# Opening of a two-block network on one core: modulation of four feature tiles and the sum of squares moved to TensorE

## The chip, the cores and the metric

The kernel runs on one core of one Trainium2 chip. The metric is the device time of one execution in microseconds. A core has TensorE (matrix products, with a separate stream of weight loads), VectorE, ScalarE, GpSimd, SyncE (SP, which here only issues loads) and 16 DMA engines that fill the on-chip memory. Products land in PSUM, eight banks of 512 fp32 columns.

## The reference, cut to what matters

Two transformer-like blocks in sequence on 256 tokens of 1024 features, fp32. Only the start of the first block is touched by the change:

```python
cond = silu(c)                                     # c: (1, 1024)
mod = (cond @ w_ada + b_ada).reshape(b, 6, d)      # w_ada: (1024, 6144)
shift1, scale1, gate1, shift2, scale2, gate2 = [mod[:, i] for i in range(6)]
hn = rmsnorm(x, norm1_g) * (1 + scale1) + shift1   # x: (1, 256, 1024)
proj = hn @ w_in                                   # split into q, k, v, index q, k, weights, gates
```

Everything behind it (index scores and top-k attention, stick-breaking attention, an expert layer that picks among 16384 rows, and the whole second block) is the same before and after.

## The kernel before, in words

Activations are held feature-major: eight tiles of 128 features by 256 tokens. Weights come in chunks of 128x1024 fp32 (512 KB) through four buffers `wraw`. Each chunk is split by `weights` (L92) into a high part, a ScalarE copy (L98), and a low part, a subtract on VectorE or GpSimd (L100); activations are split likewise. A product is then made of three: high x high, high x low, low x high. A scheduler orders each engine's instructions when the program is built, from the dependences, the order of the code and its own estimate of times; `issue_after` adds an order between two instructions of one engine. On the chip each engine follows its list.

The opening is in `first_mixer` (L284). The row c is loaded and spread over 128 partitions by two products with a column of ones (L251); after a Silu it is `cond`, 128x1024. x comes in four loads (L301), ScalarE squares it (L303), VectorE adds the squares up (L305 to L307), and one fp32 product with a matrix of ones sums over the partitions (L314). From it come `ms` and `rstd` (L326, and L169 to L174), and `xr` = x times `rstd` (L336): the first pair of tiles on VectorE, three pairs on GpSimd.

The modulation rows are made one tile of 128 output features at a time: `ada_one` (L260) loads a 128x1024 block of the transposed `w_ada` and VectorE multiplies it with `cond` and sums along the row (L266). Tile k needs two of them, row 8+k for the scale and row k for the shift. They use four buffers, two for even and two for odd tiles; those of the odd tiles share their memory (`bias1`) with the squares. VectorE then adds `b_ada` (L270) and makes the scale `gs` (L389), ScalarE makes `hn` and `y` (L393), and VectorE the low part of `hn` (L395).

The products against `w_in` are in pieces (L361, L363), so that they can start with the first tile. The string `ORDER` lists the steps: "a" makes the next tile of `hn` and multiplies it with all chunks that are there, "w" brings one of nine chunks for index q, k and their weights, and multiplies it with all tiles that are there, "v" brings one of four chunks of the value weights, each covering two tiles. `LOWS` says which of the 13 chunks have their low part made on VectorE (v) or GpSimd (g). SP issues the loads in the order of the steps and waits whenever a buffer isn't free. When all eight tiles are done, ScalarE copies the sums out (L425 to L432), and the index scores begin (L609).

Of the kernel before, what the change touches and what calls it, by code (L numbers as in the profile page):

```python
# [9 lines left out]
FT = mybir.dt.float32  # L10
# [3 lines left out]
AF = mybir.ActivationFunctionType  # L14
OP = mybir.AluOpType
# [4 lines left out]
T = 256  # L20
D = 1024
KT = 8
EPS = 1e-6
NEG = -3.0e38
TAKEN = -3.4e38
ORDER = "wwawaavavwwawavwwaawv"
LOWS = "vgvgvgvvvvvgv"
EXP_LN = 6
# [42 lines left out]
class Net:  # L71
# [15 lines left out]
    def load(self, dst, src):  # L87

        with self.tc.issue_after(self.last_load.ins) if self.in_turn else ExitStack():
            self.last_load = self.nc.sync.dma_start(dst, src)  # L90
# [152 lines left out]
    def load_cond(self, pool):  # L243

        nc = self.nc
        row = pool.tile([1, D], FT, name="crow")
        nc.sync.dma_start(row, self.ap["c"])
        self.cond = pool.tile([128, D], FT, name="cond")
        pss = [self.ps([128, 512], "mm") for _ in range(2)]
        for z, ps in enumerate(pss):  # L250
            nc.tensor.matmul(ps, self.ones[0:1, :], row[:, 512 * z:512 * z + 512], start=True, stop=True)  # L251

        def finish():
            for z, ps in enumerate(pss):
                self.last_act = nc.scalar.activation(self.cond[:, 512 * z:512 * z + 512], ps, AF.Silu)
            self.condd = self.dram.tile([1, D], FT, name="condd")
            nc.scalar.dma_start(self.condd, self.cond[0:1, :])
        return finish

# [24 lines left out]
    def first_mixer(self):  # L284
        nc, tc, ap = self.nc, self.tc, self.ap
        with ExitStack() as es:
# [10 lines left out]
            self.table = self.act_table(SILU)  # L297
            cond = self.load_cond(A)
            sq = P.tile([128, KT, T], FT, name="sqs", tag="bias1")
            for k in range(0, KT, 2):  # L300
                nc.sync.dma_start(x[:, k:k + 2], ap["x"][:, k:k + 2])  # L301
                with tc.issue_after(self.table):
                    high = nc.scalar.activation(sq[:, k:k + 2], x[:, k:k + 2], AF.Square)  # L303
                if k % 4:
                    nc.vector.tensor_add(sq[:, k - 2:k], sq[:, k - 2:k], sq[:, k:k + 2])  # L305
            nc.vector.tensor_add(sq[:, :2], sq[:, :2], sq[:, 4:6])
            pair = nc.vector.tensor_add(sq[:, 0], sq[:, 0], sq[:, 1])  # L307
            with tc.issue_after(high.ins):
# [3 lines left out]
            nc.scalar.dma_start(self.b_ada, self.ap["b_ada"])  # L312
            ps = self.ps([128, T], "sm")
            nc.tensor.matmul(ps, self.ones, sq[:, 0], start=True, stop=True)  # L314
            r = P.tile([128, T], FT, name="rstd")
            n1 = Scratch(P.tile([128, 3 * T], FT, name="norm1", tag="kx"))
            ms = n1.tile([128, T], FT, name="ms")
            rows = [Scratch(P.tile([128, 2 * D], FT, name=f"ada{i}", tag=t)) for i, t in enumerate(("sgb", "bias1"))]

            def ada_row(k, j):  # L320
                self.ada_one(A, j, rows[k % 2].tile([128, D], FT, name="ada", bufs=2))

            with tc.issue_after(pair.ins):
                ada_row(0, 8)
            with tc.issue_after(self.last_ada.ins):
                mean = nc.vector.tensor_scalar(ms, ps, 1.0 / D, EPS, op0=OP.mult, op1=OP.add)  # L326
            with tc.issue_after(mean.ins):
                ada_row(0, 0)
            with tc.issue_after(self.last_ada.ins):
                self.rsqrt(n1, r, ms, [128, T])  # L330
# [3 lines left out]
            xr = P.tile([128, KT, T], FT, name="xr", tag="sga")  # L334
            for k in range(0, KT, 2):
                (nc.gpsimd if k else nc.vector).tensor_tensor(  # L336
                    xr[:, k:k + 2], x[:, k:k + 2], r[:, None, :].to_broadcast([128, 2, T]), op=OP.mult)

# [8 lines left out]
            f = F.__enter__()  # L347
# [6 lines left out]
            vacc = [self.ps([128, 512], "acc") for _ in range(2)]  # L354
            nlow = iter(LOWS)

# [25 lines left out]
            for e in ORDER:  # L382
                if e == "a":
                    k = known
                    if k:
                        ada_row(k, 8 + k)
                        ada_row(k, k)
                    self.ada_end(k, k + 1)
                    nc.vector.scalar_tensor_tensor(self.gs[:, 0, k:k + 1], self.mod[:, 8 + k:9 + k],  # L389
                                                   self.vecs[:, 0, k:k + 1], bg[:, k:k + 1], op0=OP.mult, op1=OP.add)  # L390
# [14 lines left out]
                with tc.issue_after(norm_exp.ins), tc.issue_after(self.last_rsqrt.ins):  # L405
                    w = self.weights(ap["w_in"][len(first) if e == "w" else 9 + c], next(nlow),
                                     spare.pop() if e == "w" else None)
# [1031 lines left out]
def _col(v):  # L1439
    return v.reshape(-1, 128).T  # L1440
# [10 lines left out]
def prepare(inputs):  # L1451
    i = {k: np.asarray(v) for k, v in inputs.items()}
    ar = np.arange
    o = {}
    o["x"] = i["x"][0].T.reshape(8, 128, 256).transpose(1, 0, 2)
    o["mem"] = i["mem_2"][0].T.reshape(8, 128, 256).transpose(1, 0, 2)
    o["c"] = i["c"]
    o["w_ada"] = i["w_ada"][0].T.reshape(48, 128, 1024)
    o["b_ada"] = _col(i["b_ada"][0])
    o["vecs"] = np.stack([_col(v) for v in (  # L1460
# [57 lines left out]
```

## Time and profile before

| what | value |
|---|---|
| median of 3 runs | 1452.14 us (1450.41 to 1454.54) |
| the profiled execution | 1451.56 us, span 1449.8 us |
| TensorE busy | 1382.8 us (95%) |
| VectorE busy | 1102.9 us (76%) |
| ScalarE busy | 756.3 us (52%) |
| GpSimd busy | 151.3 us (10%) |

All times of the rows are counted from the start of the span. "Busy" is the share of time in which an engine has an instruction at work; a product and the weight load of the next one overlap. In a row of the timeline the first number is the start, the second the time from the start of the first to the end of the last instruction merged into it, then engine, line, operation, output<-inputs, shape and count. In a row of the table of stretches stand its bounds and length, the busy time (and count of instructions) of TensorE's products, its weight loads, VectorE, ScalarE and GpSimd, the granted clock of TensorE, the share of the DMA engines and what they moved in GB/s. In the timeline, what stands in square brackets is how long the engine had been idle, and what ended that.

### The profile page before, as it was taken

What the parts mean: (1) busy time and instruction counts of PE and PEld (TensorE: products, weight loads), DVE (VectorE), ACT (ScalarE), POOL (GpSimd) and SP (SyncE); (2) the same over time, 40 slices, a digit from 0 to 9 for tenths busy, and PEclk for the clock granted to TensorE, in tenths of its full rate; (3) what the DMA queues carried; (4) which work ended last, traced back from release to release, by engine and by line L of the source; (5) the groups of instructions that cost most, each with busy time, mean ns of one, the idle gap of its engine ahead of it and who ended that gap; (6) DMA issues with size and microseconds to landing.
All of it is one profiled execution on the core that took longest, in us unless ns stands there. A gap on an engine that the chain in (4) does not pass through costs nothing. (4 is left out here: it accounts for less than half of the span.)

```text
span 1449.8 us, 28871 instructions
## 1 busy us (share of the span) xinstructions
PE 1382.8 (95%) x11584; PEld 1326.8 (92%) x11584; DVE 1102.9 (76%) x2082; ACT 756.3 (52%) x1358; POOL 151.3 (10%) x64
## 2 busy tenths in 40 slices
PE   4989899999898999999999999999999999899997
PEld 2879799899898999999999999999999879799996
DVE  7797988549999888999856556665557796777776
ACT  4546664455445555555554444444445465655555
POOL 3100000018995000000000000000000000000001
PEclk9999999999999999999999999999999999999998
DMA  7766776655555545545566666776664444266662
GB/s 278 268 202 230 267 243 200 207 186 156 169 186 161 168 153 166 166 151 171 152 207 221 198 189 192 240 233 201 186 188 141 148 123 157 74 189 191 192 193 94
DMA packets 76234, 269.51 MB, mean 186 GB/s; under 512 B 8970, under 2 KB 11202, under 8 KB 75460
## 3 DMA queue, kind: packets, MB, share of 16 engines
q1 hardware_dynamic: 71426, 257.99, 55.6%
q10 hardware_dynamic: 4674, 9.69, 2.0%
q8 instruction: 90, 1.47, 0.4%
q14 instruction: 44, 0.36, 0.1%
HBM read 265.01 MB, written 4.21 MB: 186 GB/s over the span
## 5 line engine op out<-in xcount | busy, mean ns | idle before, releaser
L98 ACT ACTIVATE wh<-wraw 128x1024 fp32r<-128x1024 f32 x431 | 456.3, 1061 | 522.8 <-PE ps_acc L130 244.1
L100 DVE TENSOR_TENSOR wl<-wraw,wh 128x1024 fp32r<-128x1024 f32 x384 | 470.3, 1227 | 253.9 <-ACT wh L98 251.1
L129 PE MATMUL ps_acc<-c,wh 128*128 128x256 f32 x1024 | 286.6, 280 | 0.0
L130 PE MATMUL ps_acc<-c,wh 128*128 128x256 f32 x1024 | 286.5, 280 | 0.0
L131 PE MATMUL ps_acc<-c,wl 128*128 128x256 f32 x1024 | 286.5, 280 | 0.0
L131 PE MATMUL ps_mm<-hn,wl 128*128 128x256 f32 x680 | 190.1, 280 | 9.8 <-DVE wl L100 7.1
L131 PE MATMUL ps_acc<-hn,wl 128*128 128x256 f32 x696 | 192.5, 277 | 4.7 <-POOL wl L100 4.7
L129 PE MATMUL ps_mm<-hn,wh 128*128 128x256 f32 x680 | 192.6, 283 | 2.7 <-ACT wh L98 2.6
L129 PE MATMUL ps_acc<-hn,wh 128*128 128x256 f32 x696 | 193.9, 280 | 0.0
L129 PEld LDWEIGHTS ps_acc<-c,wh 128*128 128x128 f32 x1024 | 192.5, 188 | 0.1
L131 PEld LDWEIGHTS ps_acc<-c,wl 128*128 128x128 f32 x1024 | 192.5, 188 | 0.0
L130 PEld LDWEIGHTS ps_acc<-c,wh 128*128 128x128 f32 x1024 | 192.5, 188 | 0.0
L130 PE MATMUL ps_acc<-hn,wh 128*128 128x256 f32 x696 | 192.4, 277 | 0.0
L130 PE MATMUL ps_mm<-hn,wh 128*128 128x256 f32 x680 | 189.5, 279 | 0.0
L131 PEld LDWEIGHTS ps_mm<-hn,wl 128*128 128x128 f32 x680 | 128.2, 189 | 11.6 <-DVE wl L100 8.6
L100 POOL TENSOR_TENSOR wl<-wraw,wh 128x1024 fp32r<-128x1024 f32 x47 | 131.8, 2826 | 56.4 <-ACT wh L98 56.2
L131 PEld LDWEIGHTS ps_acc<-hn,wl 128*128 128x128 f32 x696 | 130.8, 188 | 5.4 <-POOL wl L100 5.4
L129 PEld LDWEIGHTS ps_mm<-hn,wh 128*128 128x128 f32 x680 | 128.9, 190 | 5.2 <-ACT wh L98 3.3
L130 PEld LDWEIGHTS ps_acc<-hn,wh 128*128 128x128 f32 x696 | 130.7, 188 | 0.2 <-DVE hn L281 0.2
L129 PEld LDWEIGHTS ps_acc<-hn,wh 128*128 128x128 f32 x696 | 130.4, 188 | 0.4 <-ACT hn L280 0.2
L130 PEld LDWEIGHTS ps_mm<-hn,wh 128*128 128x128 f32 x680 | 128.5, 189 | 0.2
L1404 POOL TENSOR_TENSOR big<-big 128x512 f32<-128x512 f32 x4 | 5.0, 1265 | 981.8 <-DVE big L1401 981.8
(484 smaller groups left out, 2770.9 us busy)
## 6 DMA issues: line engine op xcount, KB each, us to landing
wraw<-in_peer_u_dram SPq DMA_DIRECT2D x128, 512.0 KB, 4.0
wraw<-in_peer_v_dram SPq DMA_DIRECT2D x128, 512.0 KB, 4.4
wraw<-in_w_in_dram SPq DMA_DIRECT2D x70, 512.0 KB, 4.8
wraw<-in_ffn_up_dram SPq DMA_DIRECT2D x44, 512.0 KB, 3.6
wraw<-in_ffn_down_dram SPq DMA_DIRECT2D x22, 512.0 KB, 3.6
ada<-in_w_ada_dram SPq DMA_DIRECT2D x16, 512.0 KB, 6.0
wraw<-in_w_out_dram SPq DMA_DIRECT2D x16, 512.0 KB, 4.6
wraw<-in_peer_wq_dram SPq DMA_DIRECT2D x16, 512.0 KB, 3.6
```

The source lines that it names most:

```text
L98: nc.scalar.activation(h, raw, AF.Copy)
L100: (nc.vector if eng == "v" else nc.gpsimd).tensor_tensor(l, raw, h.bitcast(FT), op=OP.subtract)
L129: mm(out, a[0], b[0], start=first, stop=False, **kw)
L130: mm(out, a[0], b[1], start=False, stop=False, **kw)
L131: self.last_mm = mm(out, a[1], b[0], start=False, stop=last, **kw)
L1404: nc.gpsimd.tensor_tensor(xf[:, tb, cs], xt[:, tb, cs], fg[:, cs], op=OP.mult)
```

## The change

- The eight modulation rows of tiles 0 to 3 (the constant `ADA_PE`) are made on TensorE: their blocks of `w_ada` are stored in the other orientation, and each row is eight accumulating fp32 products, with the block as weights and one column of `cond_col`, repeated 64 times, as the moving operand. The results stand in one PSUM bank, 64 columns each; VectorE reads the first column. Tiles 4 to 7 stay on VectorE.
- The squares are summed by eight fp32 products with the matrix of ones that accumulate in the same bank (its first 256 columns, which tiles 2 and 3 use afterwards), in place of VectorE's adds and one product. The squares use another buffer (`hm1`).
- The conditioning row comes twice: as columns (128x8) on ScalarE's queue, and as a load that repeats it over 128 partitions, behind x on SP's queue, in place of two products.
- GpSimd's share goes to VectorE: the low parts of four chunks, and three pairs of `xr`, which are now made one pair at a time in the even "a" steps.
- `ORDER` is another one.

```diff
--- before.py
+++ after.py
@@ -23,8 +23,8 @@
 EPS = 1e-6
 NEG = -3.0e38
 TAKEN = -3.4e38
-ORDER = "wwawaavavwwawavwwaawv"
-LOWS = "vgvgvgvvvvvgv"
+ORDER = "awwawawawwvvaawwvwaav"
+ADA_PE = 4
 EXP_LN = 6
 SILU = 18
 PLAN = "ijjaavaasvqvqvksskkssksqssrgrqsssrgss0gr1rggr0rrrgrg1rg20g31rg2rrg3rrgg23rg"
@@ -243,19 +243,22 @@
     def load_cond(self, pool):
 
         nc = self.nc
-        row = pool.tile([1, D], FT, name="crow")
-        nc.sync.dma_start(row, self.ap["c"])
+        col = pool.tile([128, KT], FT, name="ccol")
+        nc.scalar.dma_start(col, self.ap["c_col"])
+        self.cond_col = pool.tile([128, KT], FT, name="cond_col")
+        with self.tc.issue_after(self.table):
+            nc.scalar.activation(self.cond_col, col, AF.Silu)
         self.cond = pool.tile([128, D], FT, name="cond")
-        pss = [self.ps([128, 512], "mm") for _ in range(2)]
-        for z, ps in enumerate(pss):
-            nc.tensor.matmul(ps, self.ones[0:1, :], row[:, 512 * z:512 * z + 512], start=True, stop=True)
+        c = self.ap["c"]
+
+        def load():
+            nc.sync.dma_start(self.cond, bass.AP(tensor=c.tensor, offset=c.offset, ap=[[0, 128], [1, D]]))
 
         def finish():
-            for z, ps in enumerate(pss):
-                self.last_act = nc.scalar.activation(self.cond[:, 512 * z:512 * z + 512], ps, AF.Silu)
+            self.last_act = nc.scalar.activation(self.cond, self.cond, AF.Silu)
             self.condd = self.dram.tile([1, D], FT, name="condd")
             nc.scalar.dma_start(self.condd, self.cond[0:1, :])
-        return finish
+        return load, finish
 
     def ada_one(self, pool, j, w=None):
         nc = self.nc
@@ -295,46 +298,58 @@
             self.upper = P.tile([128, 128], FT, name="upper")
             nc.vector.tensor_scalar(self.upper, self.relx[:, 128:], 0.0, None, op0=OP.is_gt)
             self.table = self.act_table(SILU)
-            cond = self.load_cond(A)
-            sq = P.tile([128, KT, T], FT, name="sqs", tag="bias1")
+            load_cond, cond = self.load_cond(A)
+            rows = [Scratch(P.tile([128, 2 * D], FT, name=f"ada{i}", tag=t)) for i, t in enumerate(("sgb", "bias1"))]
+            ps = self.ps([128, 2 * T], "sm")
+            mods = ps.rearrange("p (a b) -> p a b", b=64)
+
+            def mod_at(k, j):
+
+                return (k + 2) % 4 * 2 + j // 8
+
+            def ada_row(k, j):
+                w = rows[k % 2].tile([128, D], FT, name="ada", bufs=2)
+                if k >= ADA_PE:
+                    return self.ada_one(A, j, w)
+                self.load(w, self.ap["w_ada"][j])
+                for i in range(KT):
+                    with tc.issue_after(bank.ins):
+                        nc.tensor.matmul(mods[:, mod_at(k, j)], w[:, i * 128:i * 128 + 128],
+                                         self.cond_col[:, i:i + 1].to_broadcast([128, 64]),
+                                         start=k == 2 and j == 10 and i == 0, stop=i == KT - 1, skip_group_check=True)
+
+            sq = P.tile([128, KT, T], FT, name="sqs", tag="hm1")
             for k in range(0, KT, 2):
                 nc.sync.dma_start(x[:, k:k + 2], ap["x"][:, k:k + 2])
                 with tc.issue_after(self.table):
                     high = nc.scalar.activation(sq[:, k:k + 2], x[:, k:k + 2], AF.Square)
-                if k % 4:
-                    nc.vector.tensor_add(sq[:, k - 2:k], sq[:, k - 2:k], sq[:, k:k + 2])
-            nc.vector.tensor_add(sq[:, :2], sq[:, :2], sq[:, 4:6])
-            pair = nc.vector.tensor_add(sq[:, 0], sq[:, 0], sq[:, 1])
+                for i in (k, k + 1):
+                    with tc.issue_after(bank.ins) if i else ExitStack():
+                        m = nc.tensor.matmul(ps[:, :T], self.ones, sq[:, i], start=i == 0, stop=i == KT - 1,
+                                             skip_group_check=True)
+                    bank = bank if i else m
+            load_cond()
             with tc.issue_after(high.ins):
                 cond()
             self.table = self.act_table(EXP_LN, self.last_act)
             nc.scalar.dma_start(self.vecs, self.ap["vecs"])
             nc.scalar.dma_start(self.b_ada, self.ap["b_ada"])
-            ps = self.ps([128, T], "sm")
-            nc.tensor.matmul(ps, self.ones, sq[:, 0], start=True, stop=True)
             r = P.tile([128, T], FT, name="rstd")
             n1 = Scratch(P.tile([128, 3 * T], FT, name="norm1", tag="kx"))
             ms = n1.tile([128, T], FT, name="ms")
-            rows = [Scratch(P.tile([128, 2 * D], FT, name=f"ada{i}", tag=t)) for i, t in enumerate(("sgb", "bias1"))]
-
-            def ada_row(k, j):
-                self.ada_one(A, j, rows[k % 2].tile([128, D], FT, name="ada", bufs=2))
-
-            with tc.issue_after(pair.ins):
-                ada_row(0, 8)
-            with tc.issue_after(self.last_ada.ins):
-                mean = nc.vector.tensor_scalar(ms, ps, 1.0 / D, EPS, op0=OP.mult, op1=OP.add)
+            mean = nc.vector.tensor_scalar(ms, ps[:, :T], 1.0 / D, EPS, op0=OP.mult, op1=OP.add)
+            ada_row(0, 8)
+            ada_row(0, 0)
             with tc.issue_after(mean.ins):
-                ada_row(0, 0)
-            with tc.issue_after(self.last_ada.ins):
                 self.rsqrt(n1, r, ms, [128, T])
             norm_exp = self.last_exp
             bg = P.tile([128, KT], FT, name="bg")
             nc.vector.scalar_tensor_tensor(bg, self.b_ada[:, 8:16], 1.0, self.vecs[:, 0], op0=OP.add, op1=OP.mult)
             xr = P.tile([128, KT, T], FT, name="xr", tag="sga")
-            for k in range(0, KT, 2):
-                (nc.gpsimd if k else nc.vector).tensor_tensor(
-                    xr[:, k:k + 2], x[:, k:k + 2], r[:, None, :].to_broadcast([128, 2, T]), op=OP.mult)
+
+            def scaled(k):
+                nc.vector.tensor_tensor(xr[:, k:k + 2], x[:, k:k + 2], r[:, None, :].to_broadcast([128, 2, T]),
+                                        op=OP.mult)
 
             hn = self.hi_lo("hn0")
             qi = P.tile([128, 4, T], FT, name="qi", tag="qx")
@@ -352,7 +367,6 @@
             spare += [[f.tile([128, D], FR, name=f"w0{i}{j}") for j in range(2)] for i in range(3)]
             banks = [self.ps([128, 2, T], t) for t in ("acc", "acc", "mm", "mm", "sm")]
             vacc = [self.ps([128, 512], "acc") for _ in range(2)]
-            nlow = iter(LOWS)
 
             def product(bank, out, l, r, last):
 
@@ -385,8 +399,12 @@
                     if k:
                         ada_row(k, 8 + k)
                         ada_row(k, k)
-                    self.ada_end(k, k + 1)
-                    nc.vector.scalar_tensor_tensor(self.gs[:, 0, k:k + 1], self.mod[:, 8 + k:9 + k],
+                    if k % 2 == 0:
+                        scaled(k)
+                    on_pe = k < ADA_PE
+                    shift, scale = (mods[:, mod_at(k, j), :1] if on_pe else self.mod[:, j:j + 1] for j in (k, 8 + k))
+                    nc.vector.tensor_add(self.mod[:, k:k + 1], shift, self.b_ada[:, k:k + 1])
+                    nc.vector.scalar_tensor_tensor(self.gs[:, 0, k:k + 1], scale,
                                                    self.vecs[:, 0, k:k + 1], bg[:, k:k + 1], op0=OP.mult, op1=OP.add)
                     y = P.tile([128, T], FT, name="y1", bufs=2)
                     for t in (hn[0][:, k], y):
@@ -403,7 +421,7 @@
                     continue
                 c = len(parts)
                 with tc.issue_after(norm_exp.ins), tc.issue_after(self.last_rsqrt.ins):
-                    w = self.weights(ap["w_in"][len(first) if e == "w" else 9 + c], next(nlow),
+                    w = self.weights(ap["w_in"][len(first) if e == "w" else 9 + c], "v",
                                      spare.pop() if e == "w" else None)
                 if e == "w":
                     i = len(first)
@@ -1455,7 +1473,10 @@
     o["x"] = i["x"][0].T.reshape(8, 128, 256).transpose(1, 0, 2)
     o["mem"] = i["mem_2"][0].T.reshape(8, 128, 256).transpose(1, 0, 2)
     o["c"] = i["c"]
+    o["c_col"] = _col(i["c"][0])
     o["w_ada"] = i["w_ada"][0].T.reshape(48, 128, 1024)
+    pe = [j + k for j in (0, 8) for k in range(ADA_PE)]
+    o["w_ada"][pe] = o["w_ada"][pe].reshape(-1, 128, 8, 128).transpose(0, 3, 2, 1).reshape(-1, 128, 1024)
     o["b_ada"] = _col(i["b_ada"][0])
     o["vecs"] = np.stack([_col(v) for v in (
         i["norm1_g"][0], i["norm2_g"][0], i["final_g"], i["norm_mix_g_2"][0], i["norm_xattn_g_2"][0],
```

## Rows read from the trace of the kernel before

**Rows 1.** The profile page, section 1: busy us, share of the span and instructions
```profile
PE 1382.8 (95%) x11584; PEld 1326.8 (92%) x11584; DVE 1102.9 (76%) x2082; ACT 756.3 (52%) x1358; POOL 151.3 (10%) x64
```

**Rows 2.** Table of stretches: stretch, length, busy us by engine, TensorE's granted clock, DMA.
```profile
10.00:35.00 25.00, 11.35 (x33) 8.21 (x34) 23.88 (x36) 9.25 (x15) 11.35 (x5) 1.00 0.77 279
35.00:69.00 34.00, 33.09 (x238) 30.69 (x238) 25.92 (x38) 19.47 (x29) 4.90 (x2) 1.00 0.78 281
70.00:130.00 60.00, 54.47 (x419) 49.42 (x416) 53.44 (x135) 31.57 (x74) 0.00 (x0) 1.00 0.58 191
```

**Rows 3.** Waits of 0 to 70 us: who for whom, total us, times, longest.
```profile
ACT hn L393 <- DVE mod L270: 24.2, 7, 7.3
```

**Rows 4.** Timeline, from the first product to the first tile of hn.
```profile
2.49 3.75 PE L251 MATMUL ps_mm<-crow,ones 1*128 1x512 f32 x4 [2.49 <-DMA crow<-in_c_dram]
...
8.17 1.07 ACT L255 ACTIVATE cond<-ps_mm 128x512 f32<-128x512 f32 x2
...
9.26 1.28 ACT L161 ACT_TABLE_LOAD   x1
...
12.44 0.42 ACT L169 ACTIVATE norm<-norm 128x256 f32<-128x256 f32 x1 [1.90 <-DVE norm L326]
...
14.38 0.42 DVE L174 SCALAR_TENSOR_TENSOR rstd<-norm 128x256 f32<-128x256 f32 x1
...
17.64 0.60 ACT L393 ACTIVATE hn<-xr,mod,gs 128x256 fp32r<-128x256 f32 x1 [1.50 <-DVE xr L336]
```

**Rows 5.** Timeline, the second tile of hn and the last products of the stage.
```profile
25.70 0.22 DVE L389 SCALAR_TENSOR_TENSOR gs<-mod,vecs,bg 128x1 f32<-128x1 f32 x1
...
26.02 0.60 ACT L393 ACTIVATE hn<-xr,mod,gs 128x256 fp32r<-128x256 f32 x1 [7.29 <-DVE mod L270]
...
27.15 0.42 DVE L395 TENSOR_TENSOR hn<-y,hn 128x256 fp32r<-128x256 f32 x1
...
63.18 2.87 PE L361 MATMUL ps_sm<-hn,w 128*128 128x256 f32 x23
...
65.88 2.00 PE L361 MATMUL ps_acc<-wh,hn 128*128 128x512 f32 x8
...
67.72 1.07 PE L361 MATMUL ps_acc<-wl,hn 128*128 128x512 f32 x4
```

**Rows 6.** Timelines of weight loads and products, and two stretches of the table.
```profile
29.51 0.33 PEld L361 LDWEIGHTS ps_acc<-wh,hn 128*128 128x128 f32 x1
...
41.70 0.19 PEld L363 LDWEIGHTS ps_mm<-hn,w0yb 128*128 128x128 f32 x1
...
319.67 6.63 PE L800 MATMUL ps_acc<-big 128*128 128x128 f32 x58
...
1098.96 3.27 PEld L188 LDWEIGHTS ps_sm<-big 128*128 128x128 f32 x20
...
320.00:326.00 6.00, 6.00 (x56) 6.00 (x55) 4.40 (x30) 4.89 (x9) 2.82 (x2) 1.00 0.63 199
...
1100.00:1102.00 2.00, 2.00 (x13) 2.00 (x12) 1.64 (x2) 0.49 (x2) 0.00 (x0) 0.54 0.75 213
```

**Rows 7.** Instructions of VectorE: ns min/median/max and starts (first), mean ns (second).
```profile
L266 DVE SCALAR_TENSOR_TENSOR junk<-ada,cond x16: 1212/1220/3368, 10.6 to 56.5; 128x1024 f32<-128x1024 f32 x16
...
L306 DVE TENSOR_TENSOR sqs<-sqs 128x512 f32<-128x512 f32 x1 | 0.7, 687 | 0.0
```

**Rows 8.** Two stretches of the table (GB/s last), and a broadcast load, us to landing.
```profile
0.00:10.00 10.00, 3.75 (x4) 1.16 (x4) 2.73 (x9) 5.52 (x8) 0.74 (x6) 1.00 0.77 261
10.00:20.00 10.00, 2.23 (x5) 1.22 (x5) 9.89 (x16) 5.30 (x8) 5.12 (x3) 1.00 0.96 363
...
big<-in_final_g_dram ACTq DMA_DIRECT2D x1, 512.0 KB, 5.6
```

**Rows 9.** Waits of SP's queue, 0 to 70 us.
```profile
SPq L90 <- DVE junk L266: 11.9, 5, 7.4
...
SPq L90 <- PE ps_sm L314: 5.9, 1, 5.9
```

## The prediction, made before the changed kernel was run

> **What bounds the kernel now.** I read the page's head first: TensorE is busy for 1382.8 us, 95% of the span, so time is to be had only where TensorE starves [rows 1]. The table of stretches says where: 11.35 us busy out of 25 between 10 and 35 us, then 33.09 of 34 until 69 us, while VectorE is busy for 23.88 of those 25 and GpSimd for 11.35 [rows 2]. The waits name the link: ScalarE's `hn` waits 24.2 us in 7 turns for VectorE's `mod` [rows 3]. The first of the eight tiles of `hn` begins at 17.64 us, the second at 26.02, and the last product of the stage ends at 67.72 + 1.07 = 68.8 [rows 4, 5]. So the opening is bound by VectorE's modulation rows up to 35 us and by TensorE's backlog behind it.
>
> The backlog: 9 weight chunks x 8 tiles x 3 products = 216 of 256 columns, and 48 of 512 columns for v. A run of 23 takes 2.87 us, the last one 0.28 of it, so one each 0.118 us; a run of 8 of the long ones takes 2.00, so 0.23 each [rows 5]. 216 x 0.118 + 48 x 0.23 = 36.5 us. Between 18.3 us (first product) and 68.8 lie 50.5 us: 14 us went to waits and to the low clock.
>
> **The clock.** The clock column reads 1.00 in the opening as well [rows 2], but a weight load at 29.5 us lasts 0.33 us and one at 41.7 us 0.19 [rows 6]. I go by the loads: the low level (1.2 GHz) first, the high one (2.4 GHz) from some point between.
>
> **The change, part by part.**
>
> *VectorE.* Removed: eight rows at 1.22 + 0.08 = 10.4 us; adds over the squares, three at 0.69 and one of half the size, 2.4. Added: four low halves, bounded by the row's 1.22 of the same size, 4.9; three `xr` pairs at 0.69, the price of an add of two operands of that size, 2.1 [rows 7]. One row took 3.37 us where the median is 1.22 [rows 7]; it ran beside a GpSimd subtract, and such excesses go as well (here 2.1 us, at least nothing). Net -8 us: VectorE, 23.88 of 25 us busy now, no longer sets the pace.
>
> *Sum of squares.* It becomes 8 fp32 products of two passes each. Passes of 512 columns at the low clock come at (3.75 - 1.09) / 3 = 0.89 us, 1.09 being their mean [rows 4], so 256 columns cost 0.44, at the high level half. The x loads are issued 0.4 us earlier, since the row c stood before them in SP's queue for that long; the Silu, directly behind the last square, began at 8.17 [rows 4], so the last square ends at 7.8 and, with 1.15 us between the four, the first at 4.35. All low: 4.35 + 16 x 0.44 = 11.4; all high, waiting for the last pair: 8.7. I take 10.2.
>
> *Conditioning row.* c's columns go out on ScalarE's queue ahead of `vecs` and `b_ada` and delay these by 0.4 us; nothing needs them for 10 us. The broadcast is 0.52 MB behind x in SP's queue. A load of the same form later landed in 5.6 us [rows 8]; issued near 2.5 us it lands between 7.2 (by bytes) and 9.8, I take 8.8. Silu (1.07) and table load (1.28) follow [rows 4], so Ln can't begin before 11.4. From Ln's start to the end of `rstd` took 14.38 + 0.42 - 12.44 = 2.36: `rstd` at 13.8, `xr` at 14.5, then 0.32 from the scale to `hn` [rows 5] and 0.15 for the shift: first `hn` at 15.0 instead of 17.64. A broadcast 1 us late makes that 1 us later.
>
> *Modulation on TensorE.* 8 rows x 8 products x 2 passes = 128 passes. No row shows 64 columns, but both neighbours are there. With 128 columns 58 passes take 6.63 us, (6.63 - 0.28) / 57 = 0.111 each; with 2 columns 20 take 3.27 with the clock halved about midway, so 10 p + 10 x 2 p = 3.27 and p = 0.109 [rows 6]. The load of the weights sets both, so I take 0.112: 1.8 us a row, 14.3 us in all; at the low level twice that, 28.6 us.
> This row bears on a sentence of the Trainium skill (TensorE: Matmul & The Clock Gate, Part 3, "The mechanism"): weight loads overlap running products only where the row groups differ. By it a 64-column pass would cost load and stream, by my estimate 0.112 + 0.053, so 21 us for the 128, and the stage would end 2 us later than now. The rows speak against it, 128 columns costing no more than 2, so I give it no chance of its own.
>
> *When the rows arrive.* SP's queue stood 5.9 us behind the sum of squares (shared buffer) and 7.4 behind VectorE's rows [rows 9]; the first goes with the new buffer, the second with VectorE's load. 2.6 MB were in at 10 us and 6.2 at 20 [rows 8], which in the new order are the rows of tile 0 and of tile 2; tile 1 lies between, at 16.2. At 400 GB/s from there, tile 3 follows at 24.2, the last v chunk before tile 4 at 29.4, tile 7 at 45. A row's buffer is free when TensorE has used the row two tiles before, each time before the queue gets there.
>
> *The sum on TensorE*, which takes its instructions in one order: rows of tile 0 from 10.2 to 13.8. The next rows go into the same PSUM bank that VectorE reads; whether a write waits for that read isn't shown, it costs 0 to 0.4 us a tile and I take 0.4, nearly the 0.32 from scale to `hn` [rows 5]. Tile 1: from 15.0, second row there at 16.2, done 18.6; six products 0.7: 19.3. Tile 2: 19.7 + 3.6 = 23.3, twelve products 1.4: 24.7. Tile 3: 25.1 + 3.6 = 28.7, 18 products 2.1: 30.8. Left: 36.5 - 36 x 0.118 = 32.3 us, whose operands all arrive in time (tile 7 at 45): 63.1. From 35 to 69 us TensorE now misses 0.9 of 34 us [rows 2]; I add 0.9. The stage ends at 64.0 instead of 68.8: 4.8 us gained. Saturated from 10.2 on it would be 10.2 + 14.3 + 36.5 = 61.0: 7.8.
>
> *Behind it.* From 70 to 130 us TensorE is busy for 54.47 of 60 us and VectorE for 53.44 [rows 2]; both start from this stage's outputs, so the shift passes on whole. The profiled execution took 1451.56 us; 1451.56 - 4.8 = 1446.8. The median of the runs is 0.58 above it: 1447.3.
>
> **Rivals.**
> *A, the turns on TensorE.* If the rows of the next tile stand behind the products of this one, TensorE waits out scale, `hn`, `y` and the low half, from 25.70 to 27.15 + 0.42 = 1.9 us a tile [rows 5], not 0.4: 3 x 1.5 = 4.5 us, and almost nothing is gained: 1451.8. For it: the code lists the products of a tile ahead of the next rows. Against: the order is planned over all of them, and TensorE is kept busy for 33.09 of 34 us by just that.
> *B, the clock falls in the modulation passes: slower.* The run of 2-column passes began at 1098.96 us, and the granted clock of 1100 to 1102 is 0.54, falling to the 1.2 GHz level; the 128-column run kept 1.00 [rows 6]. What 64 columns do no row tells. If all passes run low they cost 28.6 - 14.3 = 14.3 us more, and the 36 products between them double, 4.2: 1447.3 + 18.5 = 1465.8; if half do, 1456.6. It decides from a third of the passes on (4.8 / 14.3), three of the eight rows.
> The Trainium skill calls the low level the array's default, which activity releases (same page, Part 1); if the chip counts these passes as too little, that is B with its times.
> *C, the gain is taken back behind the stage.* VectorE is busy for 53.44 of 60 us from 70 to 130 us [rows 2], and relief in the opening doesn't shorten its work there. If half is lost, 1449.7. Against: that work hangs on `qi` and `ki`, which come earlier.
>
> **How the numbers follow.** Forecast 0.52 (1444.3, saturated, to 1447.8), A 0.22, C 0.12, B 0.14. 0.3% is 4.4 us, about what a measurement of this kernel can tell: under 1447.8 is faster. Faster 0.52; same 0.34 (A and C); slower 0.14 (B). The range goes from 1443.3, a us under the saturated case, over C and A to 1453.0, a us above A, and leaves out most of B.
>
> **What would show it.** First `hn` near 15 us, tiles 1 to 3 near 19, 24 and 29; modulation passes 0.11 us apart with loads of 0.19; no VectorE row of over 2 us; last product of the stage near 64 us. Wrong, if loads of 0.33 run through the modulation (B), if TensorE waits some 2 us a tile for `hn` (A), or if the stage ends early and the span doesn't follow (C).

## The result, and the profile after

The changed kernel takes 1464.4 us (median of 5 runs, 1461.8 to 1470.4), the kernel before on the same chip 1454.3 (5 runs): a ratio of 1.0081, 95% interval [1.0064, 1.0097]. It is 10 us slower by the medians and 12 by the ratio, where 5 us less were forecast, and lies above the range's upper end of 1453.0. The profiled execution is the longest of the five (1470.41 us); what is read from it below is the place of the loss, and its size is taken from the stage, not from the whole run.

The same three stretches as in [rows 2], of the changed kernel (stretch, length, busy us of TensorE, its weight loads, VectorE, ScalarE and GpSimd, granted clock, DMA share, GB/s), then stretches of 5 us:

```profile
10.00:35.00 25.00, 22.53 (x117) 21.46 (x117) 8.74 (x17) 9.48 (x12) 0.00 (x0) 0.65 0.73 281
35.00:69.00 34.00, 33.52 (x193) 31.93 (x193) 22.09 (x40) 13.06 (x18) 0.00 (x0) 0.76 0.72 261
70.00:130.00 60.00, 52.94 (x375) 46.84 (x374) 42.74 (x108) 29.79 (x57) 0.00 (x0) 0.97 0.51 160
10.00:15.00 5.00, 4.17 (x32) 3.65 (x31) 1.28 (x3) 3.75 (x5) 0.00 (x0) 1.00 1.03 417
15.00:20.00 5.00, 3.62 (x21) 3.37 (x20) 4.26 (x8) 3.11 (x5) 0.00 (x0) 0.73 1.01 401
30.00:35.00 5.00, 5.00 (x26) 5.00 (x25) 0.00 (x0) 0.00 (x0) 0.00 (x0) 0.50 0.44 178
45.00:50.00 5.00, 5.00 (x25) 5.00 (x25) 3.07 (x6) 3.31 (x5) 0.00 (x0) 0.50 0.57 188
50.00:55.00 5.00, 5.00 (x32) 4.67 (x30) 4.96 (x9) 0.72 (x2) 0.00 (x0) 0.86 0.71 235
```

Two things changed places. VectorE, 23.88 us busy out of 25 in [rows 2], now has 8.74 and does nothing at all from 30 to 35. TensorE is busy nearly all the time, at half its clock: the granted clock reads 1.00 until the modulation of the second tile begins, then 0.50. The records of the clock have one low spell there, from 17.3 to 51.4 us, in which TensorE is busy for 33.4 of 34.1 us. A busy share near 100% beside a granted clock of 0.50 is the sign to look for: the engine is full and slow.

The timeline, in the places of [rows 4] and [rows 5] (start, us, engine, line, operation; in brackets the idle time before it and what ended it):

```profile
10.58 1.06 ACT L258 ACTIVATE cond<-cond 128x1024 f32<-128x1024 f32 x1 [1.49 <-DMA cond<-in_c_dram]
...
11.95 3.76 PE L317 MATMUL ps_sm<-cond_col,ada 128*128 128x64 f32 x32 [0.83 <-DMA ada<-in_w_ada_dram]
...
12.95 0.42 ACT L169 ACTIVATE norm<-norm 128x256 f32<-128x256 f32 x1
...
15.95 0.41 DVE L174 SCALAR_TENSOR_TENSOR rstd<-norm 128x256 f32<-128x256 f32 x1
16.28 1.22 DVE L100 TENSOR_TENSOR w<-wraw,w 128x1024 fp32r<-128x1024 f32 x1
17.41 0.68 DVE L351 TENSOR_TENSOR xr<-x,rstd 128x512 f32<-128x512 f32 x1
...
18.13 0.60 ACT L411 ACTIVATE hn<-xr,mod,gs 128x256 fp32r<-128x256 f32 x1 [1.37 <-DVE xr L351]
...
27.05 2.65 PE L317 MATMUL ps_sm<-cond_col,ada 128*128 128x64 f32 x12
...
30.67 4.36 PE L317 MATMUL ps_sm<-cond_col,ada 128*128 128x64 f32 x20
...
80.27 1.09 PE L375 MATMUL ps_acc<-wl,hn 128*128 128x512 f32 x4
...
81.17 1.09 ACT L450 ACTIVATE va<-ps_acc 128x512 f32<-128x512 f32 x2 [0.30 <-PE ps_acc L375]
82.14 1.06 ACT L98 ACTIVATE wh<-wraw 128x1024 fp32r<-128x1024 f32 x1
```

The first 32 modulation passes, at the high level, come (3.76 - 0.28) / 31 = 0.112 us apart (0.28 is the last pass itself); at the low level a run of 20 takes 4.36 and one of 12 takes 2.65: (4.36 - 2.65) / 8 = 0.214. The stage's last product ends at 81.4 instead of 68.8. Half of the 34.1 us at the low level is 17.0 us; 81.4 - 17.0 = 64.4, beside the 64.0 of the forecast. The waits (for whom, us in total, times, longest) have turned round against [rows 3]: `hn` still waits, but VectorE's `mod` and `gs` now wait for TensorE's passes (L317).

```profile
DVE mod L406 <- PE ps_sm L317: 22.3, 4, 9.4
ACT hn L411 <- DVE gs L407: 22.0, 3, 9.3
ACT hn L411 <- DVE mod L406: 12.7, 4, 4.5
```

### The profile page after: what moved, and what is told of

It is laid out like the page before. It is cut to its first block, busy times and chain, and to the rows that moved or that the text cites. A ratio compares the mean times of both kernels' runs of the same rounds, so it can differ in the third digit from the quotient of the medians.

```text
span 1468.6 us, 29123 instructions
## 1 busy us (share of the span) xinstructions
PE 1416.7 (96%) x11722; PEld 1365.0 (93%) x11722; DVE 1084.4 (74%) x2069; ACT 757.1 (52%) x1358; POOL 135.3 (9%) x57
## 5 line engine op out<-in xcount | busy, mean ns | idle before, releaser
L100 POOL TENSOR_TENSOR wl<-wraw,wh 128x1024 fp32r<-128x1024 f32 x46 | 129.3, 2832 | 51.4 <-ACT wh L98 51.3
```

The costliest lines, as they stand in the source:

```text
L100: (nc.vector if eng == "v" else nc.gpsimd).tensor_tensor(l, raw, h.bitcast(FT), op=OP.subtract)
```

## Experiments

Two times are used to place a gain: the start of the copies of v (`va`, 69.0 us in the kernel before), with which the stage ends, and the start of the squares of `mem` (`sq` at L195, which the expectations call the first squares of the attention), before which the planned turns of attention lie. Between them is "the stretch behind the stage". From the squares to the end the profiled executions of all thirteen kernels need 1306 to 1313 us (time less start of the squares: 1451.56 - 141.2 = 1310.4 before, 1470.41 - 157.1 = 1313.3 after), while the squares themselves begin between 134.3 and 157.1 us: most of the differences arise ahead of them. The 7 us of spread behind them, in single executions, don't follow the edits.

Behind the stage `wh` and `wl` are the high and the low part of a weight chunk, `rel` is the index scores as ScalarE takes them out of PSUM, and VectorE adds them up (the index adds) and picks the largest (topk). The string `PLAN` lists the turns in which the work there is written, "a" for a block of queries `qa`, "i" and "j" for the index scores.

**128 columns.** The operand of the modulation passes is twice as wide, and two tiles instead of four share the bank in turn. Each pass is also set behind the one before it in TensorE's order; the planner then spreads the products of the finished tiles a little differently between the passes. All else is as in the change. (In the diffs, `...` stands for lines left out.)

```diff
-mods = ps.rearrange("p (a b) -> p a b", b=64)
+mods = ps.rearrange("p (a b) -> p a b", b=128)
+mm = [None, None]
...
-return (k + 2) % 4 * 2 + j // 8
+return (k + 1) % 2 * 2 + j // 8
...
-with tc.issue_after(bank.ins):
+with tc.issue_after(mm[0] or bank.ins):
...
-self.cond_col[:, i:i + 1].to_broadcast([128, 64]),
-start=k == 2 and j == 10 and i == 0, ...
+self.cond_col[:, i:i + 1].to_broadcast([128, 128]),
+start=k > 0 and j == 8 + k and i == 0, ...
...
+mm[0] = m.ins
```

> The changed kernel with 128 columns in each modulation product instead of 64 (all else alike, the results lie 128 apart in the bank, two tiles by turns). Theory 1, the clock: the products of 64 columns let TensorE fall to 1.2 GHz from 17 to 51 us, and that is the whole loss. With 128 columns the rows of the kernel before show the clock held at the same 0.11 us a pass; then the granted clock stays 1.00 from about 10 us, the four modulation tiles end near 14, 19, 24 and 29 us, the stage's last product near 65 (now 81.4), and the time is 1446 to 1451 us, below the kernel before (1454). Rival, the work itself: 128 passes on TensorE and the turns between tiles are what costs; then the stage ends at 76 us or later and the time stays at 1460 or more. Rival, the columns cost: passes of 128 columns take twice as long, 0.22 us at the high clock: the stage ends near 78 us.

Measured: 1451.4 us, 0.9990 [0.9978, 1.0002] of before. Three stretches of this kernel:

```profile
10.00:35.00 25.00, 23.57 (x194) 22.40 (x193) 16.32 (x29) 14.32 (x19) 0.00 (x0) 1.00 1.00 387
75.00:80.00 5.00, 2.15 (x12) 1.65 (x11) 4.55 (x14) 0.48 (x2) 0.00 (x0) 1.00 0.55 117
80.00:90.00 10.00, 8.12 (x41) 7.53 (x41) 6.43 (x12) 3.58 (x5) 0.00 (x0) 0.56 0.85 271
```

Its timeline, from the modulation of the third tile to the first wait behind the stage:

```profile
22.85 2.39 PE L318 MATMUL ps_sm<-cond_col,ada 128*128 128x128 f32 x20
...
63.62 1.09 ACT L453 ACTIVATE va<-ps_acc 128x512 f32<-128x512 f32 x2 [0.30 <-PE ps_acc L378]
64.59 1.06 ACT L98 ACTIVATE wh<-wraw 128x1024 fp32r<-128x1024 f32 x1
...
78.44 1.22 DVE L100 TENSOR_TENSOR wl<-wraw,wh 128x1024 fp32r<-128x1024 f32 x1
79.71 0.38 PE L131 MATMUL ps_mm<-hn,wl 128*128 128x256 f32 x1 [2.85 <-DVE wl L100]
```

The clock reads 1.00 from 9.5 us, where its record begins, to 81.1, behind the stage; passes come (2.39 - 0.28) / 19 = 0.111 us apart, and the stage ends at 63.6: 17.6 us earlier than with 64 columns, which is the half of 34.1 and 0.5 more. So the low level in the opening is what the change lost its time to, and it goes with the width of the passes; the new order of the passes was not tried without the width. But of the 5.4 us that the stage now wins over the kernel before, the run keeps 1, which the interval doesn't tell from nothing. The timeline says where they go: TensorE waits 2.85 us for a split of weights that VectorE does behind a row of index adds and a topk; 1.4 us behind that wait the low level comes, for 10.2 us, and products that took 0.114 us take 0.21. The stretch behind the stage takes 79.1 us instead of 72.2.

**8 columns**, the opposite direction, one execution:

```diff
-nc.tensor.matmul(mods[:, mod_at(k, j)], ...
-self.cond_col[:, i:i + 1].to_broadcast([128, 64]),
+nc.tensor.matmul(mods[:, mod_at(k, j), :8], ...
+self.cond_col[:, i:i + 1].to_broadcast([128, 8]),
```

> The changed kernel with 8 columns in each modulation pass instead of 64; the rest of the change is kept. Theory 1 (these passes leave TensorE at the 1.2 GHz level because they stream little beside their loads): the granted clock reads 0.50 from about 17 us until the modulation is over, as with 64 columns; the passes come at 0.21 us each there, no faster than with 64, since the load sets the price; the v copy of this stage begins near 81 us as with 64 columns (81.2), and the time is near 1464 us. Rival (the low spell came from something else in the opening, such as the position of the waits, and the columns do not matter): the spell's length changes freely and the v copy begins nearer to 64 us, where 128 columns had it. A second rival (64 columns cost stream time beside the load): the passes come closer together than 0.21 us at the low level.

Measured: 1461.9 us; low from 14.8 us for 23.9 and from 42.1 for 6.8, `va` at 79.0 us. Two runs of its timeline at the low level give (3.42 - 0.43) / 14 = 0.214 us a pass, what 64 columns cost there: the load sets the price, as theory 1 had it, and the low time is about as long (30.7 us together against 34.1). The last two rows speak against the rival by which the place of a wait brings the low level: from 38.72 to 42.13, at the high level, TensorE was busy for 3.41 of 3.41 us, most of it with passes of 8 columns, and at 42.13, within the second row, the low level came back.

```profile
26.43 3.42 PE L317 MATMUL ps_sm<-cond_col,ada 128*128 128x8 f32 x16
30.91 0.43 PE L317 MATMUL ps_sm<-cond_col,ada 128*128 128x8 f32 x2
...
38.90 1.85 PE L317 MATMUL ps_sm<-cond_col,ada 128*128 128x8 f32 x16
...
41.03 2.42 PE L317 MATMUL ps_sm<-cond_col,ada 128*128 128x8 f32 x16
```

**All rows on VectorE.** Squares on TensorE, broadcast, no GpSimd and the new order stay:

```diff
-ADA_PE = 4
+ADA_PE = 0
```

> The changed kernel with no modulation tile on TensorE (all 16 rows on VectorE again); squares on TensorE, conditioning row by a transfer, no GpSimd and the new order stay. Theory 1 (only the modulation's low clock costs): no loss is left, 1448 to 1456 us, with the low clock ending near 30 to 35 us as before. Rival: if the order or the squares on TensorE are a part of the loss, 1458 or more.

Measured: 1451.8 us, 1.0001 [0.9986, 1.0015]. `va` at 64.3, the squares of `mem` at 142.0. Theory 1 holds in the time, no loss against the kernel before is left; that the order costs too shows only below. The stage is nearly as early as with 128 columns, so moving modulation to TensorE isn't what makes it early; and the gain is lost in the stretch again, 77.7 us.

**Two tiles on TensorE** instead of four, with 64 columns:

```diff
-ADA_PE = 4
+ADA_PE = 2
```

> The changed kernel with two modulation tiles on TensorE instead of four. Theory 1: the low spell is about half as long (17 us to some 32), so about half of the 10 us is lost: 1456 to 1461 us. Rival, the work itself: also about half. Rival, order or squares: as the changed kernel, 1464. If two tiles bring a gain (under 1452), the clock falls only in the later tiles.

Measured: 1450.8 us, 0.9991 [0.9977, 1.0005], less than any of the three theories gave; and the clock didn't fall later for it, as the last sentence had it. Low from 17.2 to 34.2 us, half of the spell of the change, but not half of the loss; `va` at 66.5, stretch 76.6. The kernel with all rows on VectorE has a spell as long and `va` at 64.3. In their spells TensorE is busy for 14.2 and 10.5 of 17.1 us, in that of the change for 33.4 of 34.1: where TensorE waits for rows anyway, the low level costs little; it is dear where TensorE is full.

**The kernel before without GpSimd.** Nothing but its four subtracts of low halves and three `xr` products goes to VectorE:

```diff
-LOWS = "vgvgvgvvvvvgv"
+LOWS = "vvvvvvvvvvvvv"
-(nc.gpsimd if k else nc.vector).tensor_tensor(
+nc.vector.tensor_tensor(
```

> The kernel before with GpSimd's part of the opening on VectorE (four low halves and three xr pairs), nothing else. By the excess of the VectorE instructions beside GpSimd (some 9 us) against the 7 us added, a gain of 0 to 3 us: 1451 to 1454. Rival: VectorE is what bounds the opening, and seven more microseconds on it cost 3 to 6: 1457 to 1460.

Measured: 1446.8 us, 0.9959 [0.9943, 0.9975], `va` at 63.4: more gain than expected. One edit of the change, alone, brings the stage as far forward as all of them with 128 columns, and the run keeps the gain. VectorE's rows of this kernel, beside the maximum of 3368 in [rows 7]:

```profile
L266 DVE SCALAR_TENSOR_TENSOR junk<-ada,cond x16: 1212/1218/1227, 11.0 to 50.8; 128x1024 f32<-128x1024 f32 x16
```

Two costs of GpSimd in the kernel before went at once, and no run separates them. Seven of VectorE's instructions that ran beside GpSimd's took longer than others of their form, the row of 3.37 us, three splits, a scale, an `xr` and a low part of `hn`: by my estimate, from their lengths less the median of their form, 10 us together, against 6.9 that the seven moved ones add. And GpSimd's own splits took 2.4 to 2.8 us where VectorE's take 1.22, and loads of the opening waited 1.6 and 1.9 us for two of them. The waits of `hn` for `mod`, 24.2 us in [rows 3], fall to 12.4. From the kernel before, one of the long splits of VectorE (busy us, mean ns, idle time before it), and SP's waits for GpSimd in the opening (us in total, times, longest):

```profile
L100 DVE TENSOR_TENSOR w0yb<-wraw,w0yb 128x1024 fp32r<-128x1024 f32 x1 | 2.7, 2671 | 0.7 <-ACT w0yb L98 0.7
...
SPq L90 <- POOL w0vb L100: 1.9, 1, 1.9
SPq L90 <- POOL wl L100: 1.6, 1, 1.6
```

**The turns behind the stage changed.** The kernel with 128 columns, two blocks of qa before the index scores, so that VectorE's splits stand ahead of the adds:

```diff
-PLAN = "ijjaavaas...
+PLAN = "aaijjvaas...
```

> The kernel with 128 columns (1451.4 us), with the first turns of the written order behind the stage changed from i j j a a v a a s to a a i j j v a a s: two blocks of qa come before the index scores, so that VectorE's weight splits stand ahead of its index adds. Theory 2 (the 5.4 us won in the stage are given back because TensorE waits 2.9 us for a weight split behind the index adds, and runs 10.2 us at the low level after that wait): without the wait the stretch from the v copy to the first squares of the attention falls from 79.1 us to between 72 and 74, the stage still ends near 63.5, and the time is 1446 to 1447. Rival (VectorE's and ScalarE's work of that stretch bounds it, in any order): the stretch stays at 77 to 79 us and the time at 1450 to 1452.

Measured: 1452.7 us, 0.9998 [0.9983, 1.0013]; stretch 79.5 us, as the rival had it. The stage itself ended 2 us later, `va` at 65.6. The wait went, and a longer one came: a chunk of v takes a bank that ScalarE's `rel` has not left yet, because `rel` waits for VectorE's adds.

```profile
PE ps_acc L129 <- ACT rel L525: 9.2, 1, 9.2
PE ps_mm L131 <- DVE wl L100: 0.6, 1, 0.6
```

**The same turns in the kernel before without GpSimd,** the diffs of the last two experiments together:

```diff
-LOWS = "vgvgvgvvvvvgv"
+LOWS = "vvvvvvvvvvvvv"
-(nc.gpsimd if k else nc.vector).tensor_tensor(
+nc.vector.tensor_tensor(
-PLAN = "ijjaavaas...
+PLAN = "aaijjvaas...
```

> The kernel before with GpSimd's subtracts and products on VectorE (1446.8 us), with the same change of turns, a a i j j v a a s. Its stretch from the v copy to the first squares is 74.4 us, with a wait of 1.5 us for a weight split and 3.4 us at the low level. Theory 2: little is to be had there, 1445 to 1447. Rival (the turns are worth something by themselves, wherever they stand): 1442 to 1444.

Measured: 1450.8 us, 0.9978 [0.9964, 0.9992], stretch 77.0 us instead of 74.4, with the same wait for `rel`, 6.3 us. Both theories had it wrong. The turns brought nothing in either kernel: by the medians they cost 1.3 and 4.1 us, with intervals that overlap those of the same kernels without them. That these turns plan the wait behind the stage away, as theory 2 had it, falls.

**128 columns with the order of the kernel before.**

```diff
-ORDER = "awwawawawwvvaawwvwaav"
+ORDER = "wwawaavavwwawavwwaawv"
```

> The kernel with 128 columns (1451.4 us), but with the order of tiles and weights of the kernel before in the opening (w w a w a a v a v w w w a ... instead of a w w a w a w a ...). Theory 3 (the new order leaves ScalarE's and VectorE's weight splits one weight row further back at the end of the stage, 64.6 us for the split that the kernel without GpSimd does at 62.3, and this starts the wait behind the stage): the stage ends later, 65 to 67 us, since the first products wait for weights, but the stretch behind falls from 79.1 to 72 to 75 us: 1447 to 1449. Rival (the order is innocent): stretch 78 to 79 us, 1451 to 1454.

Measured: 1447.8 us, 0.9959 [0.9943, 0.9976]. The stage ends at 66.5, 2.9 us later than with the new order, and the stretch behind takes 71.2 us instead of 79.1: theory 3. In ScalarE's timeline the copy of v and the next split of weights stand the other way round than in the change and with 128 columns, where `wh` came behind `va`:

```profile
65.44 1.06 ACT L98 ACTIVATE wh<-wraw 128x1024 fp32r<-128x1024 f32 x1 [0.70 <-PE ps_acc L378]
66.53 1.09 ACT L453 ACTIVATE va<-ps_acc 128x512 f32<-128x512 f32 x2
```

TensorE's two longest kinds of waits in the stretch, with 128 columns and the new order:

```profile
PE ps_mm L131 <- DVE wl L100: 4.9, 3, 2.9
PE ps_mm L129 <- ACT wh L98: 1.4, 1, 1.4
```

And in this kernel, with the old order, where the second kind is gone:

```profile
PE ps_mm L131 <- DVE wl L100: 3.5, 3, 1.5
```

In all five kernels with the new order and the old turns (the change, 128 columns, 8 columns, VectorE's rows, two tiles) the split follows `va`, the longest wait for `wl` is 2.4 to 2.9 us and that for `wh` 1.4, and 3.4 to 10.2 us of low level lie in the stretch. In the kernel before and the five that keep its order and turns (three of them below) the split precedes `va`, the longest wait is 1.5 us and that for `wh` 0.7 or none; of these only the kernel before without GpSimd has a low spell in the stretch, of 3.4 us.

**The old order with 64 columns, with VectorE's rows, and with two tiles at 128 columns.** The first differs from the change by the ORDER line alone, the second also by `ADA_PE = 0`; the third is the kernel of the experiment above (128 columns, old order) with `ADA_PE = 2`.

```diff
-ORDER = "awwawawawwvvaawwvwaav"
+ORDER = "wwawaavavwwawavwwaawv"
-ADA_PE = 4
+ADA_PE = 0
```

> The changed kernel, 64 columns kept, with the order of tiles and weights of the kernel before (w w a w a a v a v ...). Theory 4 (the columns and the order are two separate losses): the granted clock still reads 0.50 for most of the modulation, and the v copy begins at 80 us or later, but the stretch from there to the first squares of the attention is 71 to 73 us instead of 75.9: 1458 to 1461 us. Rival (the order matters only once the clock holds, since at the low level TensorE alone bounds the opening): stretch 75 to 77 us, 1463 to 1466.

> The changed kernel with all modulation rows on VectorE and with the order of tiles and weights of the kernel before; the sum of squares on TensorE, the row of the condition broadcast by a transfer and no GpSimd are kept. With the new order it took 1451.8 us, with a stretch of 77.7 us behind the stage. Theory 3 (the new order costs some 4 us behind the stage): stretch 72 to 74 us, 1446.5 to 1448.5, as the kernel before without GpSimd (1446.8). Rival (squares and broadcast cost something by themselves): 1449 to 1452.

> 128 columns, the old order of tiles and weights, and modulation rows of two tiles instead of four on TensorE. If modulation on TensorE brings something beyond taking the work off GpSimd (rival): between the neighbours with four tiles (1447.8) and none, and unlike both of them by 1 us or more. Theory (VectorE's rows are no longer what bounds the stage once GpSimd is out of the way): 1446.5 to 1448.5, no difference from four tiles, with a v copy at 63 to 67 us.

Measured: 1458.2 us, 1.0020 [1.0005, 1.0035], low for 27.3 us; 1443.4 us, 0.9936 [0.9915, 0.9956]; 1444.9 us, 0.9944 [0.9921, 0.9966]. Theory 4 holds in the stretch (72.2 us) and the time; `va` at 78.1 came earlier than it said. The second is the fastest kernel of all, 3 us below its expectation. The third, 1.6 below its own, lies between four tiles on TensorE (1447.8) and none (1443.4), unlike both by over 1 us, as the rival put it; but the sense is the opposite, each tile on TensorE costs rather than brings. The intervals of these three overlap, so that is not settled. All kernels, in us (times are medians; "low" is the time at the granted clock of 0.50, in the opening from where the record begins, 7 to 11 us in the rows without a note):

| order | modulation | low in the opening | `va` | stretch behind | low in it | squares of `mem` | time | ratio |
|---|---|---|---|---|---|---|---|---|
| old | kernel before | record begins at 35.2 | 69.0 | 72.2 | 0 | 141.2 | 1452 to 1454 | 1 |
| new | 64 columns, the change | 34.1 | 81.2 | 75.9 | 3.4 | 157.1 | 1464.4 | 1.0081 |
| new | 128 columns | 0 | 63.6 | 79.1 | 10.2 | 142.7 | 1451.4 | 0.9990 |
| new | 8 columns, one execution | 30.7 | 79.0 | 75.9 | 3.4 | 154.9 | 1461.9 | |
| new | VectorE | 17.1 | 64.3 | 77.7 | 6.8 | 142.0 | 1451.8 | 1.0001 |
| new | two tiles, 64 columns | 17.1 | 66.5 | 76.6 | 3.4 | 143.1 | 1450.8 | 0.9991 |
| old | 64 columns | 27.3 | 78.1 | 72.2 | 0 | 150.3 | 1458.2 | 1.0020 |
| old | 128 columns | 0 | 66.5 | 71.2 | 0 | 137.7 | 1447.8 | 0.9959 |
| old | VectorE | 13.7 | 63.0 | 71.4 | 0 | 134.3 | 1443.4 | 0.9936 |
| old | two tiles, 128 columns | 3.4 | 64.2 | 72.9 | 0 | 137.2 | 1444.9 | 0.9944 |
| new, other turns | 128 columns | 0 | 65.6 | 79.5 | 10.2 | 145.1 | 1452.7 | 0.9998 |
| old, other turns | VectorE, kernel before without GpSimd | record begins at 27.7 | 62.7 | 77.0 | 6.8 | 139.7 | 1450.8 | 0.9978 |
| old | VectorE, kernel before without GpSimd | record begins at 29.2 | 63.4 | 74.4 | 3.4 | 137.8 | 1446.8 | 0.9959 |

Three pairs of rows differ in the order alone; the intervals of each pair don't overlap, and the new order costs 1464.4 - 1458.2 = 6.2, 3.5 and 8.4 us (64 columns, 128, VectorE). The halves of a pair were timed in different sets of runs; by the ratios, each to the kernel before in its own set, it is 0.61%, 0.31% and 0.65%. With the old turns the stretch is the longer the more low time it has, 71.2 to 72.9 us without any and 75.9, 77.7 and 79.1 in the new order with 3.4, 6.8 and 10.2; no run changed the low time alone.

The low spell of 13.7 us in the fastest kernel can cost little: TensorE is busy for 6.4 us of it, waiting for VectorE's rows. Two of its stretches, 5.00 us of VectorE beside some 2 of TensorE:

```profile
15.00:20.00 5.00, 2.07 (x8) 1.78 (x8) 5.00 (x8) 2.44 (x4) 0.00 (x0) 0.50 1.03 410
20.00:25.00 5.00, 2.53 (x8) 1.65 (x8) 5.00 (x10) 2.04 (x3) 0.00 (x0) 0.50 0.83 261
```

Narrow passes don't bring the low level each time: in the kernel with 64 columns and the old order the last 32 ran wholly at the high one, (3.68 - 0.28) / 31 = 0.110 us apart.

```profile
42.65 3.68 PE L317 MATMUL ps_sm<-cond_col,ada 128*128 128x64 f32 x32
```

## Why the prediction was wrong, step by step

- **The step that failed: 128 passes at 0.112 us, 14.3 us in all.** The price of a pass was right at both levels (0.112, and 0.214 where 0.224 was said), and so was the pace of loads that covers 8, 64 and 128 columns alike. Wrong was the level. 94 of the 128 passes, and the products between them, ran at 1.2 GHz. That is rival B, at a chance of 0.14: its case with all passes low gave 1465.8 us, the median is 1464.4. So close a hit is partly luck: the low passes cost 94 x 0.102 = 9.6 us and not 14.3, the products some 7.5 and not 4.2, since the spell went on for 5 us behind the last pass, and the stretch behind took 3.7 us more, which B doesn't have. Its condition was right too (from a third of the passes on), and [rows 6] held the evidence on both sides: 128 columns at 1.00, 2 columns at 0.54. Between two neighbours that differ in the very thing that decides, I gave the better one most of the chance because the price per pass was the same for both. Equal prices at a given clock say nothing of the clock.
- **The stage sum** holds where the clock does: 64.0 forecast, `va` at 63.6 with 128 columns.
- **VectorE no longer sets the pace**: right (8.74 us of 25, splits of 1.22 us). But the sum credited this to modulation and squares leaving VectorE, with the excess beside GpSimd as "2.1 us, at least nothing". That looked at the rows of modulation alone; over all of VectorE's instructions it is some 10 us. The kernel before without GpSimd shows the order of size the other way round: taking GpSimd out, which adds 7 instructions to VectorE, ends the stage 5.6 us earlier by itself.
- **First `hn` at 15.0**: 18.1. The broadcast ended its wait at 10.58 instead of 8.8, and Ln followed at 12.95, 1.55 us behind the forecast. The rest is VectorE's order, which the sum left out: the last step of `rstd` stood behind `mod` and `gs`, which waited for TensorE, and `xr` behind a split of 1.22 us. With 128 columns it was 15.65 us in the first of the kernels with four tiles, 17.52 and 17.53 in the two others; the Silu of the broadcast row began at 8.68, 10.54 and 9.41 there, so part of it goes with when that transfer lands.
- **Rival A, turns on TensorE**: not seen as it was described. At the low level it was TensorE's passes that `hn` waited for, by way of `mod` and `gs`, and with 128 columns TensorE was busy for 23.57 of 25 us.
- **"The shift passes on whole"**: wrong, and rival C is right in kind. With the clock held in the opening, the new order keeps 1 of 5.4 us. The reason given against C, that the work behind comes earlier, looked at data alone; the order of the splits on ScalarE and VectorE at the seam had changed with the ORDER line, and that wasn't priced at all. C's own reason, VectorE's 53 us of work in 60, isn't it either: VectorE's busy time in the stretch is 60.1 to 60.3 us in all eleven kernels with the old turns, while the stretch takes 71 to 79.

The Trainium skill (TensorE: Matmul & The Clock Gate, Part 1, "What's actually happening") says that the low level is the default and that activity releases it. The runs agree in the direction: with four tiles the clock fell to 0.50 in the opening with 8 and with 64 columns, and stayed at 1.00 with 128.

What stays open: whether the width alone holds the clock, without the new order of the passes that came with 128 columns, and why some runs of narrow passes stayed at the high level; how much of GpSimd's cost is VectorE's longer instructions and how much its own slower ones; why one split of weights fewer stands before the copies of v with the new order follows from the planner's order and was not taken apart further; whether the wait of 2.85 us brings the low spell of 10.2 us behind it by itself was not tried alone, so that the cost of the new order is shown and its way through waits and clock is in part argued; and the 3 us between the last row of the table and the fastest kernel, whose openings differ by squares and broadcast, lie within overlapping intervals.

## What to carry to other kernels

Before moving small products to TensorE, price them at both clock levels, and look for a row of the very operand width that the edit uses; where there is none, the slow case is not the unlikely one. Take a many-part change apart by its cheapest part first: here two lines, leaving GpSimd out beside a full VectorE, gave a ratio of 0.9959 alone, as much as the whole change with 128 columns and the old order. And where an edit reorders a stage, check the seam: which splits and copies stand behind its last product, in the order that each engine will take them.

## What the runs showed of the hardware

- Passes with full 128 x 128 weights come equally far apart with 8, 64 and 128 moving columns, as long as the clock is the same: 0.214 us at the low level (8 and 64 columns), 0.112 and 0.111 at the high one (64 and 128). The width that costs nothing more is also the one that kept the high level through the opening in all three kernels with four tiles.
- The low level can come back without a pause of the engine: with 8 columns TensorE was busy for 3.41 of 3.41 us before it did.
- TensorE was shown busy for 33.4 of 34.1 us and was granted half its clock all that time.
- Beside GpSimd's work some of VectorE's instructions of the opening were longer, others not: one row of sixteen took 3.37 us and three of twelve splits 2.29 to 2.67, against at most 1.23 us for both without it.
